# One more Strassen pair a round, a deeper ring of split weights, held pieces, and moved copies and loads in a float32 encoder layer

## The chip, the cores and the metric

The kernel runs on one core of one Trainium2 chip. The metric is the time of one execution on the device in microseconds; the median of 3 runs of the kernel before is 2016.77 us (2015.5 to 2017.98).

## The reference

One encoder layer on 256 tokens of width 2048 in float32: a feed-forward half-step, a mixer (attention and a Fourier branch), and a second feed-forward half-step. The change touches the two feed-forward blocks, and one place behind the first of them.

```python
def _swiglu(x, w_gate, w_up, w_down):
    return (jax.nn.silu(x @ w_gate) * (x @ w_up)) @ w_down

def _macaron_ffn(x, pre_g, w_gate, w_up, w_down, post_g):
    return x + MACARON_WEIGHT * _rms_norm(_swiglu(_rms_norm(x, pre_g), w_gate, w_up, w_down), post_g)
...
    h = _macaron_ffn(h, ffn1_pre_g[l], ffn1_w_gate[l], ffn1_w_up[l], ffn1_w_down[l], ffn1_post_g[l])
    h = _gated_mixers(h, ...)
    h = _macaron_ffn(h, ffn2_pre_g[l], ffn2_w_gate[l], ffn2_w_up[l], ffn2_w_down[l], ffn2_post_g[l])
```

D_MODEL is 2048 and D_FF is 5632, so each of `w_gate`, `w_up`, `w_down` holds 46 MB.

## The kernel before

**A product in three matmuls.** A float32 operand is split into a high and a low part: ScalarE (ACT) writes `whi`, the rounded value, and VectorE (DVE) writes `wlo`, the rest (`split`, L102 and L103). `mm3` (L108 to L110) then runs hi×hi, lo×hi and hi×lo on TensorE (PE). A weight piece is 128 partitions × 2 × 512 columns (`WP`, `NB`), 512 KB, loaded by SyncE's queue (SP) into one of 5 `raw` buffers. Its split goes into a ring of 6 places (`wring`, tiles `whi` and `wlo`).

**A round.** The hidden width is done in 11 blocks of 512 columns; the first two (`PLAIN`) by ordinary loops, the other nine in rounds (`ffn`, the loop over `f`). A round has two stages. In the row stage, 8 pieces r1 to r8 of `w_down` are multiplied with the block before (`Rows`; 12 matmuls a piece), added to the output `y` in this way: a copy of `y` is first written to a PSUM bank (`seed`, L637), the matmuls add onto it, and `out` copies it back (L655). In the product stage, gate and up of one block are computed (`swiglu`). The 2048 rows of the weights are 16 groups of 128, in 8 pairs. A pair that is done plainly takes 2 pieces and 8 products (24 matmuls). A pair in `BY_SEVEN` is done by Strassen's method with 7 products (21 matmuls): DVE forms three differences `t` and one in place of `raw` (`minus`, L557), and 4 pieces are split (three of 1024 elements a partition and one of 512). The names in the code for them are `first`, `second`, then `ra` and the half of `t`. Pairs 0, 1, 2, 4 and 6 are done so; 3, 5 and 7 plainly. Pair 5's two plain pieces stand between and behind the pieces of pair 4.

**The order** on DVE, ACT and PE inside the rounds is that of the code (`manual_schedule`). `Line` is a queue of steps: `feed` first runs as many of the oldest steps as needed to keep fewer than `RING` in the queue, then issues the split of the new piece. So piece n+6 is split behind the matmuls of piece n and behind whatever work hangs on step n (`then`). SP's order is set by a scheduler.

**A block's end.** When the sevens are done, their sums are read out of PSUM by adds on DVE (`add`, L562), then SiLU on ACT, `times` on DVE (L574), and the copies `seed(0)` and `seed(1)` of `y` for the next row stage, which need a PSUM bank each. There are 8 banks: 5 in the pool `pmm`, 3 in `ptr`. In the next row stage, the block is transposed (`turn_h`, PE tile `pt`), once a round.

**Memory.** Pool `b8` has 12 tiles of 8 KB a partition: in the rounds 2 for `y`, 6 for the split input (`Forms`, tiles `fh` and `fl`), and 4 that, in the kernel before, take from round f = 4 on the residual and the gains for the end of the block (`tail`: tiles `h`, `gpost`, `gpre`).

**Behind the first feed-forward.** `last_rows` ends the block: it normalises (`norm.scale`, tile `c`), adds the residual (`h`, L403), multiplies (`y`, L417), transposes and begins the next projection (`col`, PE tile `pc`). The mixer's constants are loaded at the same time: `tables` (L785, L788: tiles `gcq`, `gsq`, from `rc` and `rsn`) and the DFT matrices (`dps`, `dcs`, from `draw`).

Of the kernel before, what the change touches and what calls it, by code (L numbers as in the profile page):

```python
# [18 lines left out]
P = 128  # L19
# [24 lines left out]
RING = 6  # L44
SPARE = (None, None, "chunk", "u")
# [3 lines left out]
BY_SEVEN = (0, 1, 2, 4, 6)  # L49
# [7 lines left out]
def encoder_layer(  # L57
# [384 lines left out]
    class Forms:  # L442
# [3 lines left out]
        def __init__(self, u, rs):  # L446
            self.u, self.rs, self.seven, self.plain = u, rs, {}, {}
            self.rooms, self.used = [], KD

        def put(self, src):  # L450

            out, n = [], src.shape[1]
            while len(out) < n:
                if self.used == KD:
                    self.rooms, self.used = [big("f" + c, F32R, [P, KD, P]) for c in "hl"], 0
                a = len(out)
                m = min(n - a, KD - self.used)
# [40 lines left out]

    def ring(src):
# [11 lines left out]
    class Line:  # L511


        def __init__(self):
            self.queue = []
# [17 lines left out]
    def swiglu(line, forms, w, hs, seed):  # L533
# [13 lines left out]
        def plain(pair, i, *then):  # L547
# [6 lines left out]
            line.feed(lambda: ring(raw(pair, i)[:]), use, *then)  # L554
# [22 lines left out]
        def seven(pair, between=None, *then):  # L577
# [27 lines left out]
            if between:  # L605
                between()
            line.feed(lambda: ring(h["ra"][:]), two("p1", a11, "p6", s2, end), *then[0:2])
            line.feed(lambda: ring(h["t"][:, 0:1, :]), lambda ws: mul("g1", na22, ws[0]), *then[2:])

        sums = [copy, lambda: add("x2", "p6", "x1"), lambda: add("x3", "p7", "x2"), lambda: add("x2", "p5", "x2"),  # L610
                lambda: add("x5", "p5", "x3"), lambda: seed(0)]
        gates = [lambda: add("x1", "g0", "x1"), lambda: seed(1), lambda: add("x3", "g1", "x3"),
                 lambda: silu(0), lambda: silu(1)]
        ups = [lambda: add("x2", "u0", "x2"), lambda: times(0), lambda: add("x5", "u1", "x5"), lambda: times(1)]
        for kg in range(KD // CK):
            a, b = 2 * kg, 2 * kg + 1
            if kg == KD // CK - 1:
                seven(a, None, *sums)
                plain(b, 0, *gates)
# [8 lines left out]
    class Rows:  # L628
# [5 lines left out]
        def seed(self, cb, t):  # L634
            self.ps[cb, t] = pmm.tile([P, NB], F32, tag="mm", name="pr")
# [26 lines left out]
    def ffn(u, rs, wg, wu, wgu, wd, yname, tail, gate0, w_next=None, early=()):  # L662
# [668 lines left out]
```

## Time and profile before

| what | value |
|---|---|
| median of 3 runs | 2016.77 us |
| the profiled execution, whole | 2019.0 us |
| its span | 2017.2 us |
| granted TensorE clock, mean | 0.997 |
| PE busy (matmuls) | 1997.5 us |
| DVE busy | 1707.8 us |
| ACT busy | 1323.2 us |
| the 18 rounds, from transposition to transposition | 1132.95 us |

The profiled execution is 1.8 us longer than its span, and 2.2 us above the median. In the rows of a timeline the first column is the start, the second the duration (of all instructions of the row where it ends in xN), and the bracket names the idle time of that engine before the row and what ended it. A matmul's end is modelled; the distance from start to start is what PE really takes.

### The profile page before, as it was taken

To read this page: it belongs to the slowest core of one execution; us is meant where nothing else is said; L and a number is where in the kernel's file an instruction comes from. 1 tells how busy PE (TensorE), PEld (TensorE's weight loads), DVE (VectorE), ACT (ScalarE), POOL (GpSimd) and SP (SyncE) were. 2 spreads that over 40 slices of the span, in tenths; PEclk is the share of its full clock that TensorE was granted. 3 is DMA by queue.
4 is the path that set the end of the run, shared out by engine and by line. 5 is a ranking of instruction groups with operands and counts; after the bars stand their busy time and mean duration, and the time that the engine had idled before them with its cause. 6 is when DMAs were issued, how large, how long until landed. Compare 5 with 4: busy or idle time off the path is not lost.

```text
span 2017.2 us, 25972 instructions
## 1 busy us (share of the span) xinstructions
PE 1997.5 (99%) x9200; PEld 1654.6 (82%) x9200; DVE 1707.8 (85%) x2298; ACT 1323.2 (66%) x1898; POOL 28.6 (1%) x30
## 2 busy tenths in 40 slices
PE   9999999999999999999999999999999999999998
PEld 7888888888888878888888888878888888888886
DVE  6898899988999778886877885878998898988985
ACT  7567676676766856556676564656676776676766
POOL 0000000000000010100000000000000000000002
PEclk9999999999999999999999999999999999999999
DMA  8675665556655696954555557566755666556663
GB/s 316 216 255 187 206 221 199 192 187 203 221 201 192 228 292 193 266 189 137 189 193 186 193 166 276 197 210 199 249 180 195 195 225 208 182 194 197 223 206 115
DMA packets 118738, 417.44 MB, mean 207 GB/s; under 512 B 12968, under 2 KB 19120, under 8 KB 116432
## 3 DMA queue, kind: packets, MB, share of 16 engines
q1 hardware_dynamic: 114256, 411.66, 61.1%
q0 software_dynamic: 4352, 4.13, 1.4%
q8 instruction: 72, 1.18, 0.2%
q14 instruction: 58, 0.48, 0.1%
HBM read 409.44 MB, written 6.29 MB: 206 GB/s over the span
## 4 chain that ended last, share of the span: by engine, by line
PE 89%; DVE 7%; DMA 2%; ACT 1%; issue 1%; SPq 0%; DVEq 0%; ACTq 0%
PE pc L109 17%; PE pc L108 17%; PE pc L110 17%; PE pr L108 11%; PE pr L110 11%; PE pr L109 11%; DVE wlo L103 4%; PE pt L178 2%; DMA raw<-in_f_down 1%; DVE t L557 1%; ACT whi L102 1%; DMA raw<-in_w_fo 1%; DMA rc<-in_rope_cos 0%; PE pe L108 0%; PE pe L109 0%
## 5 line engine op out<-in xcount | busy, mean ns | idle before, releaser
L103 DVE TENSOR_TENSOR wlo<-raw,whi 128x1024 fp32r<-128x1024 f32 (+1 forms) x711 | 858.2, 1219 | 163.5 <-ACT whi L102 157.0
L102 ACT ACTIVATE whi<-raw 128x1024 fp32r<-128x1024 f32 (+1 forms) x711 | 742.1, 1055 | 330.7 <-PE pc L110 120.9
L108 PE MATMUL pc<-whi,fh 128*128 128x512 f32 x1062 | 413.1, 389 | 0.0
L109 PE MATMUL pc<-wlo,fh 128*128 128x512 f32 x1062 | 413.1, 389 | 0.0
L110 PE MATMUL pc<-whi,fl 128*128 128x512 f32 x1062 | 413.1, 389 | 0.0
L109 PE MATMUL pc<-wlo,uh 128*128 128x512 f32 x688 | 270.2, 393 | 3.9 <-DVE wlo L103 3.9
L108 PE MATMUL pc<-whi,uh 128*128 128x512 f32 x688 | 272.6, 396 | 0.9 <-ACT uh L739 0.9
L108 PE MATMUL pr<-whi,hTh 128*128 128x512 f32 x688 | 270.6, 393 | 0.5 <-ACT pr L637 0.4
L110 PE MATMUL pc<-whi,ul 128*128 128x512 f32 x688 | 270.0, 393 | 0.0
L110 PE MATMUL pr<-whi,hTl 128*128 128x512 f32 x688 | 268.0, 390 | 0.0
L109 PE MATMUL pr<-wlo,hTh 128*128 128x512 f32 x688 | 267.9, 389 | 0.0
L110 PEld LDWEIGHTS pc<-whi,fl 128*128 128x128 f32 x1062 | 199.3, 188 | 41.5
L108 PEld LDWEIGHTS pc<-whi,fh 128*128 128x128 f32 x1062 | 199.4, 188 | 41.4
L109 PEld LDWEIGHTS pc<-wlo,fh 128*128 128x128 f32 x1062 | 199.3, 188 | 41.3
L102 ACT ACTIVATE whi<-t 128x1024 fp32r<-128x1024 f32 (+1 forms) x180 | 152.2, 845 | 92.0 <-DVE t L557 91.6
L103 DVE TENSOR_TENSOR wlo<-t,whi 128x1024 fp32r<-128x1024 f32 (+1 forms) x180 | 171.5, 953 | 46.0 <-ACT whi L102 46.0
L557 DVE TENSOR_TENSOR t<-raw 128x512 f32<-128x512 f32 x270 | 178.1, 687 | 3.1
L109 PEld LDWEIGHTS pc<-wlo,uh 128*128 128x128 f32 x688 | 130.0, 189 | 30.3 <-DVE wlo L103 5.2
L108 PEld LDWEIGHTS pr<-whi,hTh 128*128 128x128 f32 x688 | 129.2, 188 | 30.0 <-ACT pr L637 3.8
L108 PEld LDWEIGHTS pc<-whi,uh 128*128 128x128 f32 x688 | 130.2, 189 | 28.0 <-ACT uh L739 2.3
L110 PEld LDWEIGHTS pc<-whi,ul 128*128 128x128 f32 x688 | 130.0, 189 | 27.0
L110 PEld LDWEIGHTS pr<-whi,hTl 128*128 128x128 f32 x688 | 129.1, 188 | 27.2
(331 smaller groups left out, 2180.1 us busy)
## 6 DMA issues: line engine op xcount, KB each, us to landing
raw<-in_f_gu SPq DMA_DIRECT2D x288, 512.0 KB, 4.1
raw<-in_f_down SPq DMA_DIRECT2D x176, 512.0 KB, 5.3
raw<-in_w_in SPq DMA_DIRECT2D x112, 512.0 KB, 4.6
raw<-in_f_up SPq DMA_DIRECT2D x32, 512.0 KB, 4.6
raw<-in_w_ao SPq DMA_DIRECT2D x32, 512.0 KB, 4.0
raw<-in_w_out SPq DMA_DIRECT2D x32, 512.0 KB, 4.2
raw<-in_f_gate SPq DMA_DIRECT2D x31, 512.0 KB, 5.8
fraw<-in_w_f SPq DMA_DIRECT2D x16, 512.0 KB, 6.4
```

The lines of the kernel that those rows point to most:

```text
L102: a = A.activation(hi, src, AF.Copy)
L103: v = V.tensor_tensor(out=lo, in0=src, in1=hi.bitcast(F32), op=ALU.subtract)
L108: T.matmul(ps, lh, rh, start=first, stop=False, skip_group_check=onto)
L109: T.matmul(ps, lh, rl, start=False, stop=False, skip_group_check=onto)
L110: return T.matmul(ps, ll, rh, start=False, stop=last, skip_group_check=onto)
L178: T.transpose(pt[:, j, :], src[:, j * P:(j + 1) * P], ident[:])
L557: V.tensor_tensor(out=out, in0=a, in1=b, op=ALU.subtract)
```

## The change

- **Pair 5 joins `BY_SEVEN`**: 6 of 8 pairs by seven products. The two left over products of the split input go to a tile `frest` of another pool.
- **Ring**: while `turn["more"]` is true (rounds f = 2 to 9 from their product stage on, and the row stage of f = 10), the queue holds 10 steps, and 4 of every 10 pieces go to a `b8` tile `w2` that holds both parts. The product stage of f = 10 and all behind it has 6 places again.
- **Tail loads**: since those four tiles are in use, `tail` is called at the last round's end instead of at f = 4.
- **Hold**: `feed` keeps steps unprepared while the step executed last was marked `hold`; marked are the last two steps of the last seven pair and the first plain step of pair 7. So no new piece is split between these steps' `then` work.
- **Copies**: `seed(0)` takes a bank of `ptr` (the one that `p1` leaves) right behind the copy of `p1`, and `seed(1)` stands right behind the first add. Four items of `sums` now hang on the last seven's third piece instead of two.
- **Tables**: the 12 small DVE instructions of `tables` are placed behind the split that was issued last.

```diff
+RING_B8 = 4
-BY_SEVEN = (0, 1, 2, 4, 6)
+BY_SEVEN = (0, 1, 2, 4, 5, 6)
...
+                    if self.full <= 3:
+                        self.rooms, self.used, self.size = [big("f" + c, F32R, [P, KD, P]) for c in "hl"], 0, KD
+                    else:
+                        rest = xpool.tile([P, 4, P], F32R, tag="xt", name="frest")
...
     def ring(src):
-        hi = wring.tile([P, WP, NB], F32R, tag="hi", name="whi")
-        lo = wring.tile([P, WP, NB], F32R, tag="lo", name="wlo")
+
         n = src.shape[1]
+        i = turn["n"] = (turn["n"] + 1) % (RING + RING_B8)
+        if turn["more"] and i % 5 in (1, 3):
+            both = big("w2", F32R, [P, 2, WP, NB])
+            hi, lo = both[:, 0], both[:, 1]
+        else:
+            hi = wring.tile([P, WP, NB], F32R, tag="hi", name="whi")
+            lo = wring.tile([P, WP, NB], F32R, tag="lo", name="wlo")
         split(hi[:, 0:n, :], lo[:, 0:n, :], src)
...
-        def feed(self, ready, use, *then):
-
-            while len(self.queue) >= RING:
+        def feed(self, ready, use, *then, hold=False):
+
+
+            while len(self.queue) >= RING + RING_B8 * turn["more"]:
                 self.next()
-            self.queue.append((ready(), use, then))
+            self.queue.append([ready, use, then, hold])
+            if not self.held:
+                self.prepare()
+
+        def prepare(self):
+            for step in self.queue:
+                if step[0]:
+                    weights, step[0] = step[0](), None
+                    step[1] = lambda use=step[1], weights=weights: use(weights)
 
         def next(self):
-            b, use, then = self.queue.pop(0)
-            use(b)
+            if self.queue[0][0]:
+                self.prepare()
+            _, use, then, self.held = self.queue.pop(0)
+            use()
...
-            line.feed(lambda: ring(h["ra"][:]), two("p1", a11, "p6", s2, end), *then[0:2])
-            line.feed(lambda: ring(h["t"][:, 0:1, :]), lambda ws: mul("g1", na22, ws[0]), *then[2:])
-
-        sums = [copy, lambda: add("x2", "p6", "x1"), lambda: add("x3", "p7", "x2"), lambda: add("x2", "p5", "x2"),
-                lambda: add("x5", "p5", "x3"), lambda: seed(0)]
-        gates = [lambda: add("x1", "g0", "x1"), lambda: seed(1), lambda: add("x3", "g1", "x3"),
-                 lambda: silu(0), lambda: silu(1)]
+            line.feed(lambda: ring(h["ra"][:]), two("p1", a11, "p6", s2, end), *then[0:4], hold=end)
+            line.feed(lambda: ring(h["t"][:, 0:1, :]), lambda ws: mul("g1", na22, ws[0]), *then[4:], hold=end)
+
+        sums = [copy, lambda: seed(0, ptr, "tr"), lambda: add("x2", "p6", "x1"), lambda: seed(1),
+                lambda: add("x3", "p7", "x2"), lambda: add("x2", "p5", "x2"), lambda: add("x5", "p5", "x3")]
+        gates = [lambda: add("x1", "g0", "x1"), lambda: add("x3", "g1", "x3"), lambda: silu(0), lambda: silu(1)]
...
-                plain(b, 0, *gates)
+                plain(b, 0, *gates, hold=True)
...
-                if f == 4:
+                if f == nblk:
                     norm, nxt = tail(y)
...
+                    turn["more"] = f < nblk - 1
...
-                V.tensor_tensor(out=gc[:, t, :], in0=rc[:, t, :], in1=g[:], op=ALU.mult)
+                with tc.issue_after(latest["V"]):
+                    V.tensor_tensor(out=gc[:, t, :], in0=rc[:, t, :], in1=g[:], op=ALU.mult)
```

Three places show how instructions move. The first is DVE at a block's end in the first feed-forward, before the change; `x` are the sums, `raw` the next pieces, `t` a difference of the next block.

```order
L562 TENSOR_TENSOR x_3111<-pc,x_3109 128x512
L103 TENSOR_TENSOR wlo<-raw,whi 128x1024
L562 TENSOR_TENSOR x_3122<-pc,x_3111 128x512
L562 TENSOR_TENSOR x_3111<-pc,x_3111 128x512
L562 TENSOR_TENSOR x_3125<-pc,x_3122 128x512
L103 TENSOR_TENSOR wlo<-raw,whi 128x1024
L562 TENSOR_TENSOR x_3109<-pc,x_3109 128x512
L562 TENSOR_TENSOR x_3122<-pc,x_3122 128x512
L103 TENSOR_TENSOR wlo<-raw,whi 128x1024
L562 TENSOR_TENSOR x_3111<-pc,x_3111 128x512
```

The same engine and place with the change:

```order
L587 TENSOR_TENSOR x_3121<-pc,x_3117 128x512
L587 TENSOR_TENSOR x_3128<-pc,x_3121 128x512
L587 TENSOR_TENSOR x_3121<-pc,x_3121 128x512
L587 TENSOR_TENSOR x_3131<-pc,x_3128 128x512
L587 TENSOR_TENSOR x_3117<-pc,x_3117 128x512
L587 TENSOR_TENSOR x_3128<-pc,x_3128 128x512
L587 TENSOR_TENSOR x_3121<-pc,x_3121 128x512
L599 TENSOR_TENSOR x_3121<-x_3121,x_3117 128x512
L587 TENSOR_TENSOR x_3131<-pc,x_3131 128x512
L599 TENSOR_TENSOR x_3131<-x_3131,x_3128 128x512
L104 TENSOR_TENSOR w_3167<-raw,w_3167 128x1024
L104 TENSOR_TENSOR wlo<-raw,whi 128x1024
```

The splits of new pieces between the sums have moved behind the last of them. The second place is SP's queue in the first feed-forward before the change, from the load of the first round's `w_down` on:

```order
L83 DMA raw<-in_f_down 128x1024 x8
L83 DMA raw<-in_f_gu 128x1024 x3
L83 DMA h_1975<-in_x 128x2048
L83 DMA raw<-in_f_gu 128x1024 x2
L83 DMA h_1977<-in_x 128x2048
L83 DMA raw<-in_f_gu 128x1024 x2
L83 DMA gpost_1979<-in_f_post 128x2048
L83 DMA gpre_1981<-in_mix_pre 128x2048
L83 DMA raw<-in_f_gu 128x1024 x9
```

SP's queue with the change, from the `w_down` load of round f = 10 on:

```order
L84 DMA raw<-in_f_down 128x1024 x8
L84 DMA raw<-in_f_gu 128x1024 x3
L84 DMA h_5790<-in_x 128x2048
L84 DMA h_5792<-in_x 128x2048
L84 DMA gpost_5794<-in_f_post 128x2048
L84 DMA raw<-in_f_gu 128x1024 x2
L84 DMA gpre_5796<-in_mix_pre 128x2048
L84 DMA raw<-in_f_gu 128x1024 x11
L84 DMA raw<-in_f_down 128x1024 x16
```

The four tail loads have moved from the weights of the first round to those of the last one; each waits there for a `w2` tile that PE still reads. The third place is DVE behind the first feed-forward, before the change, from the last steps of the norm's root (`cu`, `cv`, `cr`) on:

```order
L165 TENSOR_TENSOR cu<-cz 128x1
L785 TENSOR_TENSOR gcq<-rc,gq 128x128
L166 SCALAR_TENSOR_TENSOR cv<-cu,ca 128x1
L785 TENSOR_TENSOR gcq<-rc,gq 128x128
L168 SCALAR_TENSOR_TENSOR cr<-cv,cz 128x1
L103 TENSOR_TENSOR wlo<-raw,whi 128x1024
L403 SCALAR_TENSOR_TENSOR h_1977<-y_935,cr,h_1977 128x512
L103 TENSOR_TENSOR dps<-draw,dps 128x258
L417 TENSOR_TENSOR y_935<-h_1977,gpre_1981 128x512
```

The same with the change:

```order
L166 TENSOR_TENSOR cu<-cz 128x1
L167 SCALAR_TENSOR_TENSOR cv<-cu,ca 128x1
L169 SCALAR_TENSOR_TENSOR cr<-cv,cz 128x1
L104 TENSOR_TENSOR wlo<-raw,whi 128x1024
L404 SCALAR_TENSOR_TENSOR h_5792<-y_942,cr,h_5792 128x512
L104 TENSOR_TENSOR dps<-draw,dps 128x258
L418 TENSOR_TENSOR y_942<-h_5792,gpre_5796 128x512
```

The `gcq` products have left this stretch (they stand some 40 instructions later, behind the roots `r0r` and `r1r`); the split of `dps` still stands ahead of `y`.

More of the change, by code (lines that the diff above doesn't have):

```diff
@@ L545, in raw, with plain @@
             return raw_piece(w[pair // 2], pair % 2 * 2 + i)
-        def plain(pair, i, *then):
+        def plain(pair, i, *then, hold=False):
             def use(b):
@@ L552, in use @@
                         mul("gu"[i] + str(t), forms.plain[k][t], b[j], k == KD - 1)
-            line.feed(lambda: ring(raw(pair, i)[:]), use, *then)
+            line.feed(lambda: ring(raw(pair, i)[:]), use, *then, hold=hold)
         def minus(out, a, b):
```

23 lines of the change are left out of this document (13 added, 10 removed).

## The prediction

> **What bounds the kernel now.** I read the page's head first, then the busy times by round, then the starts of single instructions inside a round, and last the waits.
>
> ```profile
> span 2017.2 us, 25972 instructions
> PE 1997.5 (99%) x9200; PEld 1654.6 (82%) x9200; DVE 1707.8 (85%) x2298; ACT 1323.2 (66%) x1898; POOL 28.6 (1%) x30
> ...
> PEclk9999999999999999999999999999999999999999
> ```
>
> PE is covered for 99% of the span, DVE for 85%, and the granted clock is full nearly everywhere. A covered PE is not yet a bound PE, since ends of matmuls are modelled, so the starts decide.
>
> ```profile
> 450.63 0.39 PE L110 MATMUL pc<-whi,fl 128*128 128x512 f32 x1
> ...
> 454.94 0.39 PE L108 MATMUL pc<-whi,fh 128*128 128x512 f32 x1
> ```
>
> These are the first and last of 20 matmuls in the product stage of a round: 4.31 us over 19 steps, so one matmul costs 0.2268 us of PE and not the 0.39 us of its row. Next the rounds, cut at their transpositions.
>
> ```profile
> core 0: us, PE busy (x) PEld busy (x) DVE busy (x) ACT busy (x) POOL busy (x), PEclk, DMA share, GB/s
> 112.08:174.88 62.80, 62.80 (x284) 52.06 (x282) 57.80 (x68) 43.54 (x55) 0.00 (x0) 1.00 0.71 244
> ...
> 300.75:363.54 62.79, 62.79 (x284) 52.07 (x282) 56.61 (x66) 43.43 (x55) 0.00 (x0) 1.00 0.59 201
> ...
> 615.46:678.48 63.02, 63.02 (x284) 52.00 (x282) 54.47 (x62) 44.35 (x57) 0.00 (x0) 1.00 0.61 209
> ...
> 1915.98:1979.26 63.28, 63.07 (x284) 52.01 (x282) 54.47 (x62) 44.24 (x57) 0.00 (x0) 1.00 0.63 204
> sum 1132.95, PE 1132.48 PEld 936.59 DVE 1017.85 ACT 784.07 POOL 0.00; mean PE 62.92 PEld 52.03 DVE 56.55 ACT 43.56 POOL 0.00
> ```
>
> A round has 32 + 35 + 24 products of three matmuls, 273 in all: 61.9 us at 0.2268, and 0.9 us is left for its 8 transpositions. So 62.79 us is PE's own time, and the 18 rounds together lie only 1132.95 − 18 × 62.79 = 2.73 us above it. The rounds are PE-bound. DVE has 56.6 us of work in 62.8.
>
> The Trainium skill ("Perfetto Trace Analysis", Identifying the Most-Contended Engine) says that matmul busy time does not tell the headroom of TensorE, and that weight-load busy time and the other engines' occupancy do; by that rule the round's 52.0 us of weight loads stand behind DVE's 56.6, DVE is the most contended engine, and a change that takes from PE and gives to DVE loses. The 0.2268 us from start to start speak against it here; it returns as the second rival.
>
> **Removed: 54 matmuls.** Pair 5 needs 21 matmuls instead of 24 in each of 18 rounds: 54 × 0.2268 = 12.2 us off PE, which is on the path. A round's PE time becomes 62.79 − 0.68 = 62.11 us.
>
> **Added: work on DVE and ACT.** The stretch of pair 4 (by seven) and pair 5 (plain) on DVE in one round:
>
> ```profile
> 446.75 1.29 DVE L557 TENSOR_TENSOR t<-raw 128x512 f32<-128x512 f32 x2
> 447.96 1.22 DVE L103 TENSOR_TENSOR wlo<-raw,whi 128x1024 fp32r<-128x1024 f32 x1
> 449.10 0.68 DVE L557 TENSOR_TENSOR raw<-raw,t 128x512 f32<-128x512 f32 x1
> 449.70 1.22 DVE L103 TENSOR_TENSOR wlo<-t,whi 128x1024 fp32r<-128x1024 f32 x1
> 450.95 0.69 DVE L557 TENSOR_TENSOR t<-raw 128x512 f32<-128x512 f32 x1
> 451.56 2.35 DVE L103 TENSOR_TENSOR wlo<-raw,whi 128x1024 fp32r<-128x1024 f32 x2
> 453.83 0.68 DVE L103 TENSOR_TENSOR wlo<-t,whi 128x512 fp32r<-128x512 f32 x1
> 454.43 1.22 DVE L103 TENSOR_TENSOR wlo<-raw,whi 128x1024 fp32r<-128x1024 f32 x1
> 455.57 1.29 DVE L557 TENSOR_TENSOR t<-raw 128x512 f32<-128x512 f32 x2
> ```
>
> From 446.75 to 455.57 are 8.82 us for one seven and two plain splits. A plain split takes (453.83 − 451.56)/2 = 1.135 us, so a seven takes 6.55, and pair 5 by seven adds 6.55 − 2.27 = 4.28 us to DVE: 60.9 us in a round of 62.1. ACT has 62.8 − 43.4 = 19 us idle in each round, and its one and a half more splits hide there. DVE's room shrinks from 6.2 to 1.2 us; whether that suffices depends on when it may work ahead, which is the ring's business.
>
> **Ring of 10, middle rounds.** PE consumes a seven in 21 × 0.2268 = 4.8 us and DVE makes one in 6.55, so in the product stage DVE falls behind and lives on what is ready at its start. Where PE and DVE stood late in the stage before the change:
>
> ```profile
> 434.33 1.23 DVE L103 TENSOR_TENSOR wlo<-t,whi 128x1024 fp32r<-128x1024 f32 x1 [1.44 <-ACT whi L102]
> ...
> 456.77 1.22 DVE L103 TENSOR_TENSOR wlo<-raw,whi 128x1024 fp32r<-128x1024 f32 x1
> ...
> 460.37 1.22 DVE L103 TENSOR_TENSOR wlo<-raw,whi 128x1024 fp32r<-128x1024 f32 x1
> ```
>
> ```profile
> 432.50 0.39 PE L108 MATMUL pc<-whi,fh 128*128 128x512 f32 x1
> ...
> 462.42 0.39 PE L108 MATMUL pc<-whi,fh 128*128 128x512 f32 x1
> ```
>
> The stage starts at 432.50. The split that ends at 435.56 is piece 6, the first one held up by the copies at the end of the row stage. The last seven is needed at 462.42 and its first piece is ready at 457.99: 4.4 us of slack; its third piece, ready at 461.59 and needed 12 matmuls later, at 465.14, has 3.55. With 10 places the piece so held up is the tenth. Counted from the stage's start: tenth piece 3.06; the rest of pairs 2 and 3, 0.61 + 3 × 1.135 + 0.60 = 4.6; two sevens 13.1; the last seven's first piece 2.43. That is ready at 23.2, and PE, after 129 matmuls, wants it at 29.3. The slack is 6 us in place of 4.4, although there is one seven more. So I charge nothing for the middle rounds.
>
> **Ring of 6, last rounds.** In the product stage of f = 10 of each feed-forward there are 6 places again but six sevens. Slack 3.55 − 4.28 − 0.68 = −1.4 us: PE waits 1.4 us there, in two rounds. Bounds: 0, if DVE enters that stage earlier, to 4, if its pieces start late.
>
> **Hold, copies.** Behind a hold nothing is split until the last plain piece is multiplied: the pieces queued behind it on DVE and ACT are r7, r8 and the next block's first two with 10 places, and r3 to r6 with 6. With 10, r1 to r6 (6 × 12 × 0.2268 = 16 us of PE) cover that. With 6, r1 and r2 cover 5.4 us, and the sums left (4 × 0.6 us) and r3's split (1.2 us) need 3.6. So hold costs nothing, and the adds and the copies come earlier. What that is worth:
>
> ```profile
> PEld pr L108 <- ACT pr L637: 3.8, 9, 0.6
> ```
>
> In 9 of 18 rounds the row stage's weight load waited for a copy of `y`, which waited for the adds. These waits make the 2.73 us. In the 16 rounds other than the last ones I take 2.73 − (0.23 + 0.49) = 2.0 us as gone. In the last two the 0.72 goes too, under the 1.4 us each: +2.1.
>
> **Tail loads.** 4 MB in the first feed-forward (3 in the second) move from the first round to the last.
>
> ```profile
> raw<-in_f_gu SPq DMA_DIRECT2D x288, 512.0 KB, 4.1
> ...
> h<-in_x SPq DMA_DIRECT2D x2, 1024.0 KB, 8.6
> ...
> gpre<-in_mix_pre SPq DMA_DIRECT2D x1, 1024.0 KB, 10.0
> ```
>
> SP now waits for PE: `gpost` for a `w2` tile that r3 frees and `gpre` for one that r5 frees, with the product stage's weights queued behind them on SP. r5 ends some 9 us before that stage (3 × 2.72 and the transpositions), and the raw pieces behind `gpre` serve the third pair, whose multiplication starts 42 × 0.2268 = 9.5 us into it; landing takes 10.0 + 4.1 and splitting 2.4, 16.5 of 18.5 us. So it fits, with 2 us to spare. Before, the same bytes in the first round (244 GB/s there against 201) cost PE nothing. I charge 0; bounds 0 and 4 us for each feed-forward.
>
> **Tables.** The one long wait of PE near the change lies behind the first feed-forward:
>
> ```profile
> 718.28 0.29 DVE L785 TENSOR_TENSOR gcq<-rc,gq 128x128 f32<-128x128 f32 x1 [3.01 <-DMA rc<-in_rope_cos]
> ...
> 720.87 0.43 DVE L103 TENSOR_TENSOR dps<-draw,dps 128x258 fp32r<-128x258 f32 x1 [0.16 <-ACT dps L102]
> 721.22 0.69 DVE L417 TENSOR_TENSOR y<-h,gpre 128x512 f32<-128x512 f32 x1
> ```
>
> ```profile
> 720.42 0.42 ACT L102 ACTIVATE dps<-draw 128x258 fp32r<-128x258 f32 x1 [8.66 <-DMA draw<-in_dft_pos]
> ```
>
> ```profile
> 720.10 0.79 PE L109 MATMUL pc<-wlo,uh 128*128 128x512 f32 x1 [3.26 <-DVE wlo L103]
> ...
> 722.83 0.83 PE L178 MATMUL pt<-ident,y 128*128 128x128 f32 x4
> ```
>
> ```profile
> 720.10:722.83 2.73, 2.73 (x7) 2.04 (x8) 2.57 (x4) 1.85 (x6) 0.00 (x0) 0.50 0.77 161
> ```
>
> DVE waits 3.01 us for `rc`, and the split behind it keeps PE waiting 3.26 us. The change takes `gcq` away, but not its neighbour: `dps` waits for its own load until 720.42 on ACT, its DVE half still stands ahead of `y`, so `y` ends at 721.9 as before. PE gets its wlo early, does six matmuls (1.4 us), and waits at the transposition of `y` until 721.9 instead of 722.83: 0.9 us gained at best. After the old wait the granted clock was 0.50 for 2.7 us, six matmuls at twice their price. The new wait is some 3.9 us long, so that slow stretch comes behind it and takes the 0.9 back. I charge 0, with bounds −0.9 and +0.9.
>
> The Trainium skill ("TensorE: Matmul & The Clock Gate", What's actually happening) puts the halved clock down to an idle window of about 3.4 us; the trace agrees (0.50 behind 3.3 us), and by that rule only a wait made clearly shorter, not one moved, would give the 1.4 us of slow matmuls back, for a sum 1.4 us lower.
>
> The split input's three more products for pair 5, once for each feed-forward, fall into the second plain block:
>
> ```profile
> 37.00:112.00 75.00, 75.00 (x338) 62.04 (x337) 62.16 (x95) 46.58 (x62) 0.00 (x0) 1.00 0.68 228
> ```
>
> PE is covered there without a gap and DVE has 13 of 75 us idle: 0, and 2 us if that cover fails.
>
> **Sum.** −12.2 − 2.0 + 2.1 + 0 = −12.1 us. The profiled execution, 2019.0 us with a span of 2017.2, would become 2006.9; from the median of the runs, 2016.77, it is 2004.6.
>
> **Rivals.** 0.2% (4 us) is about what a measurement of this kernel can tell from no change.
>
> 1. *All waits of PE in the rounds go*, because DVE enters the last rounds 1.4 us earlier: 12.2 + 2.73 + 0.9 gives 2000.9. For it: the ring is still full when f = 10 begins. Against: its product stage starts behind the same copies as before. Chance 0.13.
> 2. *DVE becomes the bound in every round.* If the 6.2 us that DVE now idles in a round come from its back-and-forth with ACT and remain, a round takes 60.9 + 6.2 = 67.1 us, 4.3 more in each of 18: 2094. The point from which it is slower than before: more than 62.8 − 60.9 = 1.9 us of DVE idle a round. For it: the rows show waits for ACT (1.44 above). Against: from 446.75 to 455.57 DVE ran without a gap, so the idle time lies where the ring was full. Chance 0.08, slower.
> 3. *The last rounds starve*, because SP stands behind PE with the tail loads: 4 us more in each feed-forward, 2012.6. For it: only 2 us to spare. Against: the first round bore the same loads. Chance 0.11, about half of it within 0.2%.
> 4. *The change doesn't do what it says*: the saved matmuls turn up as waits at each block's end, and a round stays near 62.8: 2015. Against: six microseconds of slack. Chance 0.05, within 0.2%.
>
> **Chances and range.** My forecast has 0.63. Faster: 0.63 + 0.13 + 0.06 = 0.82; within 0.2%: 0.05 + 0.05 = 0.10; slower 0.08. The forecast's own range is 2001.5 to 2009 (last rounds 0 to 4 us, tables ±0.9). The range given reaches to the first rival and to the third, 2000 to 2012.5.
>
> **What would show it.** Middle rounds of 62.1 us, with DVE near 61 and the waits of weight loads for L637's copies gone: right. Last rounds near 63.5: the −1.4 is right; 66 or more with SP behind `h` or `gpre`: the third rival. A wait for `y` of 3 to 4 us near 718 instead of one for wlo: the tables' step is right. Rounds of 64 us and more with waits for wlo all over: the second rival, and the forecast is wrong.

## Result: 6.3% slower

The changed kernel takes 2142.69 us (median of 4 runs, 2140.42 to 2148.34), the kernel before 2017.09 in the runs beside it: a ratio of 1.0628, 95% interval 1.0606 to 1.065. The prediction, 2004.6 us (2000.0 to 2012.5), was wrong in sign and in size.

The page of the changed kernel, its head and first part:

```profile
span 2146.6 us, 26154 instructions
...
PE 2032.8 (95%) x9146; PEld 1669.9 (78%) x9146; DVE 1790.8 (83%) x2416; ACT 1360.3 (63%) x1940; POOL 28.6 (1%) x30
```

PE runs 54 matmuls fewer (9146 for 9200), as planned, and yet its busy time rose from 1997.5 to 2032.8 us, while its share of the span fell from 99% to 95%. So there are waits, and matmuls that take longer. Rounds cut at their transpositions (columns: stretch and length, busy time and count of each engine, granted clock, DMA share, GB/s), and in the second row the 8 us behind one of the waits:

```profile
core 0: us, PE busy (x) PEld busy (x) DVE busy (x) ACT busy (x) POOL busy (x), PEclk, DMA share, GB/s
400.41:471.96 71.55, 65.31 (x279) 53.19 (x278) 61.21 (x72) 45.59 (x57) 0.00 (x0) 0.95 0.53 177
456.00:464.00 8.00, 5.64 (x13) 4.44 (x14) 7.18 (x10) 5.66 (x10) 0.00 (x0) 0.57 0.63 214
615.03:677.19 62.16, 62.16 (x280) 51.49 (x278) 54.13 (x64) 41.95 (x53) 0.00 (x0) 1.00 0.70 240
677.19:741.95 64.76, 63.29 (x279) 51.20 (x278) 57.92 (x69) 45.03 (x58) 0.00 (x0) 1.00 0.62 210
```

The third of these rows has no wait, and it shows PE's own time of a round: 62.16 us, the 62.11 of the prediction. It is the round in which the ring goes back from 10 places to 6 and DVE prepares little. The first row is an ordinary round: 62.16 + 3.15 of slow matmuls (65.31 − 62.16) + 6.24 without PE = 71.55. The first round of each feed-forward, in which the ring grows from 6 to 10 places, has two such waits and takes 76.3 us. The nine rounds of the first feed-forward:

```profile
112.22:741.95 629.73, 582.81 (x2503) 475.59 (x2502) 548.17 (x646) 410.64 (x517) 0.00 (x0) 0.95 0.55 188
```

629.73 us against 566.40 before (112.08 to 678.48). The second feed-forward's nine take 630.85 (1477.56 to 2108.41) against 566.55. Together that is 127.6 of the 129.4 us by which the span grew. What PE waits for there (in total, times, longest):

```profile
PE pr L109 <- ACT pr L661: 91.9, 19, 6.1
PE pt L179 <- DVE y L418: 4.1, 1, 4.1
PE pc L110 <- DVE wlo L104: 1.8, 7, 0.4
```

Not for split weights (`wlo`: 1.8 us in all) but for the copies of `y` into PSUM banks, once in most rounds. Here is one of these waits, in the rows of PE, ACT and DVE (start, duration, in brackets the idle time before and what ended it). L591 copies P1, the product that the block's sums begin with; L595 are the two silus; L661 the copies of `y`:

```profile
440.06 0.39 PE L109 MATMUL pc<-w,fh 128*128 128x512 f32 x1
...
451.86 0.39 PE L111 MATMUL pr<-whi,hTl 128*128 128x512 f32 x1
458.36 0.79 PE L109 MATMUL pr<-w,hTh 128*128 128x512 f32 x1 [6.11 <-ACT pr L661]
```

```profile
442.95 1.06 ACT L103 ACTIVATE whi<-raw 128x1024 fp32r<-128x1024 f32 x1 [2.04 <-DMA raw<-in_f_down]
...
445.21 0.58 ACT L591 ACTIVATE x<-pc 128x512 f32<-128x512 f32 x1
...
449.84 1.23 ACT L595 ACTIVATE x<-x 128x512 f32<-128x512 f32 x2 [2.04 <-DVE x L587]
...
456.76 1.06 ACT L103 ACTIVATE whi<-t 128x1024 fp32r<-128x1024 f32 x1 [2.85 <-DVE t L582]
457.72 1.10 ACT L661 ACTIVATE pr<-y 128x512 f32<-128x512 f32 x2
```

```profile
433.47 0.68 DVE L104 TENSOR_TENSOR w<-t,w 128x512 fp32r<-128x512 f32 x1
...
445.33 1.23 DVE L104 TENSOR_TENSOR w<-raw,w 128x1024 fp32r<-128x1024 f32 x1
446.48 4.53 DVE L587 TENSOR_TENSOR x<-pc,x 128x512 f32<-128x512 f32 x7
```

P1's product is complete at the latest when the next piece's matmuls begin, at 440.06. From there PE has work until 452.25 (458.36 less the wait of 6.11; the rest of the block, r1 and r2): 12.2 us of cover. But ACT copies P1 only at 445.21, 5.15 us late, because the pieces up to r6 stand ahead of that copy in its queue (on DVE they end at 446.56). And from that copy to PE's restart it takes 13.15 us: sums, silus, then the burst behind the hold, whose fourth piece waits 2.85 us on ACT for DVE's difference `t`, and only behind it the copies for the second column block. 5.15 + 13.15 is 18.3 us, 6.1 more than the cover, so PE waits, and afterwards the clock is halved for a while (the granted 0.57 of the row from 456.00).

### The profile page after: what moved, and what is told of

Same layout as the page of the kernel before. It is cut to its first block, busy times and chain, and to the rows that moved or that the text cites. A ratio compares the mean times of both kernels' runs of the same rounds, so it can differ in the third digit from the quotient of the medians.

```text
span 2146.6 us, 26154 instructions
## 1 busy us (share of the span) xinstructions
PE 2032.8 (95%) x9146; PEld 1669.9 (78%) x9146; DVE 1790.8 (83%) x2416; ACT 1360.3 (63%) x1940; POOL 28.6 (1%) x30
## 4 chain that ended last, share of the span: by engine, by line
PE 62%; DVE 25%; DMA 5%; ACT 4%; issue 3%; SPq 0%; DVEq 0%; ACTq 0%
PE pc L110 11%; PE pc L111 11%; PE pc L109 11%; DVE wlo L104 10%; PE pr L109 8%; PE pr L110 8%; PE pr L111 8%; DVE t L582 4%; DVE w L104 4%; DVE x L587 3%; DMA raw<-in_f_down 3%; ACT whi L103 2%; DVE raw L582 1%; PE pt L179 1%; ACT x L595 1%
## 5 line engine op out<-in xcount | busy, mean ns | idle before, releaser
L104 DVE TENSOR_TENSOR wlo<-raw,whi 128x1024 fp32r<-128x1024 f32 (+1 forms) x560 | 677.1, 1219 | 152.9 <-ACT whi L103 150.3
L103 ACT ACTIVATE whi<-raw 128x1024 fp32r<-128x1024 f32 (+1 forms) x560 | 585.3, 1055 | 298.6 <-PE pc L111 126.8
L109 PE MATMUL pr<-whi,hTh 128*128 128x512 f32 x492 | 206.3, 419 | 63.7 <-ACT pr L661 63.5
L110 PE MATMUL pc<-wlo,fh 128*128 128x512 f32 x626 | 244.4, 390 | 1.2 <-DVE wlo L104 1.0
L109 PE MATMUL pc<-whi,fh 128*128 128x512 f32 x626 | 243.9, 390 | 0.7 <-DVE hTl L104 0.7
L111 PE MATMUL pc<-whi,fl 128*128 128x512 f32 x626 | 243.8, 389 | 0.0
L104 DVE TENSOR_TENSOR w<-raw,w 128x1024 fp32r<-128x1024 f32 x151 | 184.3, 1220 | 29.1 <-ACT w L103 28.5
L103 ACT ACTIVATE w<-raw 128x1024 fp32r<-128x1024 f32 x151 | 159.2, 1054 | 68.7 <-DMA raw<-in_f_down 21.9
L111 PE MATMUL pr<-whi,hTl 128*128 128x512 f32 x492 | 200.9, 408 | 0.0
L110 PEld LDWEIGHTS pc<-wlo,fh 128*128 128x128 f32 x626 | 117.5, 188 | 27.9 <-DVE wlo L104 3.7
L109 PEld LDWEIGHTS pc<-whi,fh 128*128 128x128 f32 x626 | 117.5, 188 | 26.0 <-issue 0.8
```

The source lines that it names most:

```text
L103: a = A.activation(hi, src, AF.Copy)
L104: v = V.tensor_tensor(out=lo, in0=src, in1=hi.bitcast(F32), op=ALU.subtract)
L109: T.matmul(ps, lh, rh, start=first, stop=False, skip_group_check=onto)
L110: T.matmul(ps, lh, rl, start=False, stop=False, skip_group_check=onto)
L111: return T.matmul(ps, ll, rh, start=False, stop=last, skip_group_check=onto)
```

## The experiments

**The theories.** From that trace came theory A: the burst behind the hold is the cause, since it stands ahead of the copies. It fell with the first four runs, and theory E took its place: ACT and DVE run their work in the order of the code, and with R places whatever they do for a step stands behind the preparation of the piece R steps further on; a deeper ring puts more preparation ahead of the sums and copies, and a sixth seven gives DVE more to do there. The rivals: B, DVE's amount of work is the bound; C, the banks; D, the burst on DVE; G, POOL and DVE block each other; L, the loads.

### No hold

```diff
         def feed(self, ready, use, *then, hold=False):
+            hold = False
```

> The changed kernel with hold never set; ring of 10, sixth seven, banks and tables stay. Theory A (the four held pieces are prepared in one burst on ACT ahead of the copies of y for the second column block, and PE waits about 6 us for these, after which its clock is low): the rounds fall from 70-72 to 62.2-62.6 us, the last ones stay near 64.8; time 2008 to 2016 us. Rival B (DVE, with six sevens, is the bound, hold or not): rounds stay above 66 us, time above 2090. Rival C (the copies in other banks cause the wait): rounds stay near 71, 2140.

Measured: 2142.34 us, ratio 1.0609 (1.0588 to 1.0631). Nothing is won, and theory A as it stood is refuted. The time is also the one that rival C gave for the changed banks; C falls with a later version that has the same banks, no wait for a copy, and 2010.6 us. ACT's rows in a round of this kernel, and PE's wait:

```profile
367.89 0.58 ACT L592 ACTIVATE x<-pc 128x512 f32<-128x512 f32 x1
...
376.41 1.23 ACT L596 ACTIVATE x<-x 128x512 f32<-128x512 f32 x2 [4.00 <-DVE x L588]
...
379.43 1.10 ACT L662 ACTIVATE pr<-y 128x512 f32<-128x512 f32 x2
```

```profile
380.06 0.79 PE L109 MATMUL pr<-whi,hTh 128*128 128x512 f32 x1 [5.16 <-ACT pr L662]
```

The same splits now stand one by one between the sums (the silus wait 4.00 us for DVE's sums in place of 2.04), not in a burst behind them. P1's copy is as late as before, and 12.2 us follow it in place of 13.15.

### Copies of the second column block ahead of the burst

```diff
-        gates = [lambda: add("x1", "g0", "x1"), lambda: add("x3", "g1", "x3"), lambda: silu(0), lambda: silu(1)]
+        gates = [lambda: add("x1", "g0", "x1"), lambda: add("x3", "g1", "x3"), lambda: silu(0), lambda: silu(1),
+                 lambda: seed(0, cb=1), lambda: seed(1, cb=1)]
...
-                        self.seed(cb + 1, t)
+                        if (cb + 1, t) not in self.ps:
+                            self.seed(cb + 1, t)
```

> The changed kernel, hold kept; the copies of y for the second column block are issued on ACT right behind the two silus, ahead of the burst, instead of by r1's step. Theory A: the order of ACT is all, so the wait of 6 us goes though hold stays: rounds 62.2 to 63, time 2008 to 2018. Rival B: no change, above 2090. A rival D to A (DVE's burst of splits behind the release is the brake, not the copies): PE then waits for wlo of r7/r8 or for the next copies instead, rounds 66 or more, above 2080.

Measured: 2103.22 us, 1.0419 (1.0403 to 1.0435); rounds of 67.7 to 68.7 us, but for the first of each feed-forward (72.2) and the last two. A (2008 to 2018) is out, and so is B's "no change", since 39 us are won by moving two copies a round alone. D's forecast came true: PE waits for the next copies instead, in rounds above 66. The wait moved by one column block.

```profile
375.43 1.06 ACT L103 ACTIVATE whi<-t 128x1024 fp32r<-128x1024 f32 x1 [1.80 <-DVE t L582]
...
379.59 1.12 ACT L662 ACTIVATE pr<-y 128x512 f32<-128x512 f32 x2
```

```profile
380.24 0.50 PE L109 MATMUL pr<-whi,hTh 128*128 128x512 f32 x1 [3.67 <-ACT pr L662]
```

The copies for the second block are now in time. Those for the third, at 379.59, stand behind the next pieces that need `t`, and PE waits 3.67 us for them. So D's burst on DVE and the order on ACT are one cause here: theory E takes in both.

### Five sevens in the changed kernel

```diff
-BY_SEVEN = (0, 1, 2, 4, 5, 6)
+BY_SEVEN = (0, 1, 2, 4, 6)
```

> The changed kernel with pair 5 plain again: 273 matmuls a round, DVE 4.3 us less work; hold, ring of 10, banks, tables stay. Theory A: the burst is the same four pieces, so the wait stays and the round is 62.8 + 8 to 9 us: time 2140 to 2160, no faster than the changed kernel. Rival B: DVE has its room back, rounds near 62.8 and time near 2017.

Measured: 2054.5 us, 1.0183 (1.0166 to 1.02). Between both: faster by 88 us than the changed kernel, slower by 36 than the kernel before although it does the same products. A round:

```profile
374.64:439.04 64.40, 63.11 (x283) 51.99 (x282) 57.16 (x66) 43.69 (x55) 0.00 (x0) 1.00 0.59 197
```

```profile
414.82 0.58 ACT L591 ACTIVATE x<-pc 128x512 f32<-128x512 f32 x1
...
426.38 1.06 ACT L103 ACTIVATE whi<-t 128x1024 fp32r<-128x1024 f32 x1 [2.85 <-DVE t L582]
427.34 1.10 ACT L661 ACTIVATE pr<-y 128x512 f32<-128x512 f32 x2
```

```profile
427.98 0.50 PE L109 MATMUL pr<-w,hTh 128*128 128x512 f32 x1 [1.29 <-ACT pr L661]
```

The burst and its 13.16 us are the same (414.82 to 427.98), but P1 is now copied in time, and the wait shrinks to 1.29 us. So the two parts add: the burst behind the ring of 10 costs what its 13.2 us are above the cover (11.7 us here, from 414.96, where the next piece's matmuls begin, to 1.29 us before 427.98), and the sixth seven adds the delay of P1's copy. Of the 36 us, some 15 lie in the first rounds of the two feed-forwards, which take 69.5 and 71.2 us.

### A ring of 6 in all rounds

```diff
-RING_B8 = 4
+RING_B8 = 0
...
-        if turn["more"] and i % 5 in (1, 3):
+        if False:
```

> The changed kernel with a ring of 6 in all rounds, hold kept. The burst is then r3 to r6, which hold no piece that DVE must first make (no t). Theory A: the copies come behind four splits on ACT, PE waits about 1 us as in the last rounds, which had 6 places; with the 1.7 us for DVE there, rounds of 64 to 66 us: time 2030 to 2075. If hold cost the wait whatever stands in the burst: rounds of 70 and more, above 2130.

Measured: 2050.23 us, 1.016 (1.0145 to 1.0175); rounds of 64.8 us, as expected.

```profile
349.43 0.58 ACT L591 ACTIVATE x<-pc 128x512 f32<-128x512 f32 x1
...
355.48 3.88 ACT L103 ACTIVATE whi<-raw 128x1024 fp32r<-128x1024 f32 x4
359.27 1.10 ACT L661 ACTIVATE pr<-y 128x512 f32<-128x512 f32 x2
```

```profile
359.90 0.50 PE L109 MATMUL pr<-whi,hTh 128*128 128x512 f32 x1 [1.00 <-ACT pr L661]
```

The burst is four plain splits without a wait, 10.5 us from P1's copy to PE's restart. That is less than the cover, and PE waits 1.00 us only because P1's copy is late here too (the next piece's matmuls begin at 347.15, 2.3 us before it). The four places, meant to help, cost 92 us (2142.7 to 2050.2). A round is still 2.6 us above 62.16. The copies make 1.0 of that, and the rest comes with DVE: the weight loads' waits show 35.1 us for `wlo` in 59 places.

```profile
PEld pc L110 <- DVE wlo L104: 35.1, 59, 1.4
```

### Without the copies of y

```diff
-            self.w, self.rb, self.y, self.first, self.ps = w, rb, y, first, {}
+            self.w, self.rb, self.y, self.first, self.ps = w, rb, y, True, {}
+            self.write = first
...
-                for t in range(NT):
+                for t in range(NT if self.write else 0):
                     A.activation(cbs(self.y[t], cb), self.ps[cb, t][:], AF.Copy)
```

> The changed kernel (hold, ring of 10, six sevens) without the copies of y from and to the banks in all rounds but the first of each feed-forward: the row products start afresh, and their sums are lost. Theory E (the in-order queue: with 10 places, whatever ACT and DVE do for a step stands behind the preparation of a piece ten steps ahead; at a block's end DVE has that preparation still before it, and so the copies come late and PE waits for them): without the copies the waits of 5 to 6 us go, the clock stays at 1.00, rounds of 62.2 to 64 us, time 2010 to 2045. Rival B (DVE's amount of work is the bound): PE waits for wlo instead, rounds above 66, time above 2085.

Measured: 2035.23 us, 1.0089 (1.0075 to 1.0104), inside theory E's range. With all of DVE's work, the ring of 10 and the hold, 107 of the 126 us go with the copies. Their own work goes with them (ACT's busy time in a round falls from 45.6 to 36.9 us), but ACT had some 26 us of idle time in a round before. Fourteen of the 18 rounds take 62.1 to 63.7 us; the other four, 64.7 to 67.3, are longer than expected. A round, and the wait that is left, for P1's own copy:

```profile
433.25:496.83 63.58, 62.40 (x279) 51.37 (x278) 60.64 (x73) 36.89 (x41) 0.00 (x0) 1.00 0.58 200
```

```profile
PE pr L109 <- ACT x L591: 16.5, 12, 2.2
```

### The longer ring alone, on the kernel before

`ring`, the length of the queue and the tail's place as in the change:

```diff
+RING_B8 = 4
...
-            while len(self.queue) >= RING:
+            while len(self.queue) >= RING + RING_B8 * turn["more"]:
...
-                if f == 4:
+                if f == nblk:
```

> The kernel before (five sevens, no hold, its banks and tables) with a ring of 10 and the tail's loads in the last round, nothing else. Theory E: the longer ring alone makes it slower, since the sums and copies come behind pieces four steps further on: rounds of 63.5 to 65, time 2030 to 2060. If the loss with five sevens (2054.5) came from hold or from the banks: 2017, within 0.3%.

Measured: 2034.18 us, 1.0091 (1.0072 to 1.011): inside theory E's range, but not in the way it gave. Sixteen rounds take 62.8 to 63.8 us, most of them below the 63.5 to 65 expected, and 11 of the 16 us that the rounds lose lie in the first round of each feed-forward (68.1 and 68.5 us), where the ring grows. So the sign and the kind of wait are shown, and that the time fits is partly luck. In its rounds the weight loads' waits for copies have grown from 3.8 us in 9 cases to

```profile
PEld pr L109 <- ACT pr L646: 19.1, 26, 3.8
```

### The sixth seven alone, on the kernel before

```diff
-BY_SEVEN = (0, 1, 2, 4, 6)
+BY_SEVEN = (0, 1, 2, 4, 5, 6)
```

`Forms` takes `frest` as in the change.

> The kernel before (ring of 6, no hold) with the sixth pair by seven products, nothing else. If DVE's 4.3 us a round fit into its idle time, rounds of 62.1 to 62.5 and 2004 to 2011. Theory E with DVE as the bound at 6 places: rounds of 64 to 66 us as in ring_of_six, with waits for wlo; time 2035 to 2070, slower than before by more than the saved 12 us are worth.

Measured: 2118.78 us, 1.0504 (1.049 to 1.0518). Slower than theory E gave by 49 us at least. A ring of 6 without hold has splits between the sums, as in the kernel before; with DVE later, the copy that r1 needs comes late, and a halved clock, which the expectation had not counted, comes behind the wait:

```profile
434.97 0.50 PE L108 MATMUL pr<-whi,hTh 128*128 128x512 f32 x1 [2.33 <-ACT pr L642]
...
435.65 0.63 PE L110 MATMUL pr<-whi,hTl 128*128 128x512 f32 x1
436.08 0.63 PE L108 MATMUL pr<-whi,hTh 128*128 128x512 f32 x1
```

From 435.65 the matmuls start 0.43 us apart. Against this, the ring of six with hold takes 2050.2 us, 69 less; its banks, the order of its copies and its tables differ too, so the 69 us are not hold's alone.

### Hold alone, on the kernel before

`Line` as in the change, and at the three last steps but one of a block:

```diff
-            line.feed(lambda: ring(h["ra"][:]), two("p1", a11, "p6", s2, end), *then[0:2])
-            line.feed(lambda: ring(h["t"][:, 0:1, :]), lambda ws: mul("g1", na22, ws[0]), *then[2:])
+            line.feed(lambda: ring(h["ra"][:]), two("p1", a11, "p6", s2, end), *then[0:2], hold=end)
+            line.feed(lambda: ring(h["t"][:, 0:1, :]), lambda ws: mul("g1", na22, ws[0]), *then[2:], hold=end)
...
-                plain(b, 0, *gates)
+                plain(b, 0, *gates, hold=True)
```

> The kernel before (ring of 6, five sevens) with hold, nothing else. Theory E: the burst behind the hold is r3 to r6, four splits on ACT (3.9 us) ahead of the copies for the second column block; PE waits 0.1 to 1.0 us a round for these, in place of the 0.15 before: rounds of 62.8 to 63.8, time 2015 to 2036. My prediction's view (hold is free and ends the waits for copies): 2014 to 2016.

Measured: 2015.35 us, 0.999 (0.9981 to 0.9999). By the time alone this also lies at the lower edge of theory E's range, but E's 0.1 to 1.0 us of waits a round do not come, and the prediction's view holds here. A round is PE's own time, with no wait for copies left:

```profile
363.14:425.91 62.77, 62.77 (x282) 52.11 (x281) 57.06 (x67) 43.07 (x55) 0.00 (x0) 1.00 0.59 202
```

That fits the rows of the ring of six: 10.5 us from P1's copy on, when that copy is not late, lie under 11.7 us of cover.

### Two subtractions of each seven on POOL

`minus` gets the engine as an argument (VectorE unless said otherwise); the first of the two kernels has `RING_B8 = 0` too.

```diff
-minus(t[:, 1, :], rb[:, 0, :], ra[:, 1, :])
+minus(t[:, 1, :], rb[:, 0, :], ra[:, 1, :], nc.gpsimd)
...
-minus(h["t"][:, 0, :], h["ra"][:, 1, :], h["rb"][:, 1, :])
+minus(h["t"][:, 0, :], h["ra"][:, 1, :], h["rb"][:, 1, :], nc.gpsimd)
```

> The ring of 6 with hold and six sevens, and two of the subtractions of each seven (0.6 us each on DVE) on POOL, where a product of two 128x512 tensors took 1.31 us. DVE's work falls from 61.2 to some 54 us a round. Theory E, with DVE as the bound at 6 places (rounds of 64.8): rounds of 62.2 to 63, time 2006 to 2022. Rival G (POOL and DVE keep each other waiting when both read two tensors; the Trainium skill, SBUF - State Buffer, SBUF: two separate sides, states such a lock): the 12 subtractions of 1.31 us stop DVE, rounds of 66 or more, time above 2075.

> The changed kernel (ring of 10, hold) with the same two subtractions of each seven on POOL. Theory E: DVE's lag at the end of a block shrinks by more than five sevens did (rounds of 64.4 with 56.6 us of DVE), but the copies still stand behind pieces that need t: rounds of 63 to 65, time 2020 to 2055, slower than six_pool. Rival B: DVE was all, so it equals six_pool. Rival G: above 2142.

Measured: 2181.93 us, 1.0817 (1.0802 to 1.0831) with 6 places, and 2244.15, 1.1124 (1.1108 to 1.114) with 10, as rival G gave. The groups of instructions of the former, then the second group as it is in the ring of six without POOL:

```profile
L582 POOL TENSOR_TENSOR t<-raw 128x512 f32<-128x512 f32 x216 | 388.0, 1804 | 1519.1 <-DMA raw<-in_f_gu 1172.8 <-DVE wlo L104 315.2 <-PE pc L111 24.4
```

```profile
L104 DVE TENSOR_TENSOR wlo<-raw,whi 128x1024 fp32r<-128x1024 f32 x709 | 925.3, 1325 | 183.6 <-ACT whi L103 175.4 <-ACT yA L224 0.3
```

```profile
L104 DVE TENSOR_TENSOR wlo<-raw,whi 128x1024 fp32r<-128x1024 f32 x709 | 849.8, 1219 | 113.9 <-ACT whi L103 109.7 <-PE pr L111 2.0
```

A subtraction on POOL takes 1804 ns, not 1313, and DVE's splits grow from 1219 to 1325 ns on average; the longest takes 2327 ns, against 1228 without POOL. On DVE the round below is busy for 60.92 us, about as in two rounds of the ring of six without POOL (61.1 on average), although it runs 12 instructions fewer.

```profile
398.00:469.75 71.75, 65.87 (x280) 50.65 (x278) 60.92 (x61) 45.26 (x59) 21.52 (x12) 1.00 0.50 176
```

So these subtractions, moved to POOL, did not relieve DVE. How much of the loss is the mutual blocking and how much POOL's own slowness is not separated: a subtraction of 1.8 us in place of 0.6 stands in the chain of a piece too, and ACT waits 227 us in total for POOL's `t` in the kernel with 6 places.

### Half the loads

```diff
+    def half_piece(src, i):
+        raw = wraw.tile([P, WP, NB], F32, tag="raw", name="raw")
+        load(raw[:, 0:1, :], src.rearrange("p (i k c) -> p i k c", k=WP, c=NB)[:, i, 0:1, :])
+        return raw[:, 0:1, :].to_broadcast([P, WP, NB])
...
-                    line.feed(lambda i=i, cb=cb: ring(raw_piece(self.w[self.rb, cb], i)[:]),
+                    line.feed(lambda i=i, cb=cb: ring(half_piece(self.w[self.rb, cb], i)),
```

> The changed kernel with half the bytes of each piece of in_f_down loaded in the rounds (256 KB in place of 512; the other half repeats the first, so the products are of other weights), splits and matmuls as they were. In the changed kernel the copy of x1 starts 5.0 us after its product, and 4.0 us of ACT's time ahead of it are waits for loads of in_f_down. If the loads are the cause of that delay (rival L): it falls to some 2 us, PE's wait from 6.1 to 3 or less, the clock stays high, rounds of 62.5 to 66 us, time 2015 to 2075. If DVE's work is (theory E in its strict form): delay and wait stay, time 2110 to 2145.

Measured: 2092.54 us, 1.0375 (1.036 to 1.039): between both ranges, so neither rival is the whole.

```profile
427.08 0.57 ACT L596 ACTIVATE x<-pc 128x512 f32<-128x512 f32 x1
```

```profile
425.49 0.39 PE L109 MATMUL pc<-w,fh 128*128 128x512 f32 x1
...
440.56 0.50 PE L109 MATMUL pr<-w,hTh 128*128 128x512 f32 x1 [3.35 <-ACT pr L666]
```

From 427.08 to 440.56 are 13.5 us, nearly as before; P1's product was complete at 425.49, where the next piece's matmuls begin, so its copy is 1.6 us late in place of 5.15. So the loads make some 3.5 us of that delay in this round (the rows of the changed kernel show 2.04 us of it a little ahead of P1's copy), as rival L gave. But the wait is 3.35 us and not 3 or less, and the clock still falls behind most such waits: the rest is the order behind P1's copy.

### Versions with early copies, a ring of 6, and the tables put behind

The place behind the first feed-forward by itself, on the kernel before: the tables and the splits of `dps` and `dcs` are issued behind the transpositions of `y`, on ACT too.

```diff
+    with tc.issue_after(latest["A"]):
         dps = const.tile([P, 2, WE + WO], F32R, name="dps")
         split(dps[:, 0, :], dps[:, 1, :], constant(dft_pos, WE + WO)[:])
...
```

The lines up to `mid` (with `dcs`, `odd`, `first` and `alt`) stand in the same block, and the products of `tables` are placed as in the change.

> The kernel before with the tables gcq, gsq, gck, gsk and the splits of dps and dcs behind the transpositions of y, on DVE and on ACT; the rounds are untouched. PE's wait of 3.3 us behind the first feed-forward and the slow 2.7 us after it (1.4 us of loss) go: 2011 to 2014. If only the wait moves again (to h, y or uh): 2015 to 2018.

Measured: 2013.52 us, 0.9984 (0.9975 to 0.9993). No wait of PE there is longer than 0.41 us.

> Five sevens, ring of 6, hold, the changed kernel's banks, the copies of the second column block ahead of the burst, and the tables and dps behind the transpositions. Theory E: without the longer ring and the sixth seven nothing that DVE must first make stands ahead of the copies; rounds of 62.8, no waits for copies: 2008 to 2013, faster than both kernels. If hold still costs its 1.0 us a round (as in ring_of_six): 2026 to 2032.

> Like five_early_six, with six sevens: ring of 6, hold, copies of the second column block ahead of the burst, tables and dps behind the transpositions. Theory E: the 1.0 us of waits for copies a round in ring_of_six goes, and 4 us behind the first feed-forward; the waits for wlo, which DVE's amount of work sets, stay: rounds of 63.5 to 64, time 2022 to 2036, slower than five_early_six by 0.6 to 1.3%. If the sixth seven were free once the copies come early: 62.2 a round, 1998 to 2004.

Measured: with five sevens **2010.61 us, 0.9969 (0.9958 to 0.998)**, faster than both kernels; with six 2036.4, 1.0098 (1.0081 to 1.0115), 0.4 us above what was expected. The tables behind the transpositions, alone, had given 3.6 of the 6.5 us that the former gains on the kernel before, and hold alone 1.8. A round of the former and one of the latter:

```profile
363.05:425.82 62.77, 62.77 (x283) 52.09 (x281) 57.07 (x67) 43.34 (x55) 0.00 (x0) 1.00 0.59 202
```

```profile
303.41:367.29 63.88, 63.10 (x280) 51.18 (x278) 60.61 (x73) 44.15 (x58) 0.00 (x0) 1.00 0.58 196
```

Where hardly a copy is late, the sixth seven still costs (2036.4 − 2010.6)/18 = 1.4 us a round: PE saves its 0.68, and some 2.1 us come in its place, with DVE busy for 61 us in 64. The longest sum of weight loads' waits is for `wlo` (37.0 us); 6.6 us are still for the copies. This price stayed with the best order of the copies that was tried.

## Why the prediction was wrong

The eight kernels with and without each part, in us (the four with a star have the change's banks and tables too):

| | 5 sevens | 6 sevens |
|---|---|---|
| 6 places, no hold | 2017.1 (before) | 2118.8 |
| 6 places, hold | 2015.4 | 2050.2* |
| 10 places, no hold | 2034.2 | 2142.3* |
| 10 places, hold | 2054.5* | 2142.7* (the change) |

- *Removed: 54 matmuls.* Right: the round without waits takes 62.16 us.
- *Added: work on DVE.* The amount was right (busy 61.2 us against the 60.9 forecast), but not that 1.2 us of room would do with a ring that lets it work ahead. No kernel with six sevens came below 2035, and with 6 places and no hold the sixth seven alone cost 102 us. The rule of the Trainium skill ("Perfetto Trace Analysis", Identifying the Most-Contended Engine), by which the prediction found DVE the engine to spare, gave the right sign here. It is no test of the rule, which names the share of peak FLOPs (MFU) beside weight-load time for TensorE, and the prediction left that out.
- *Ring of 10, middle rounds, charged 0.* **This is the step that failed.** Its 6 us of slack are in the trace: the last seven's first piece is ready at 429.95 and wanted at 435.98, its last at 434.15 (433.47 + 0.68) and 440.06. But they are the slack of the pieces, and DVE isn't free in them. It goes on with pair 7's pieces and r1 to r6 (and waits 0.88 and 1.87 us for ACT in between, which waits for loads), and the sums, which with 10 places stand behind r6, start at 446.48. The prediction followed the split weights through the ring and did not ask where in the same queues the sums and copies stand. What the step put at nothing is the larger part of the loss: with hold and six sevens the four places cost 92 us.
- *Hold, copies.* Right with 6 places and five sevens (no wait for a copy is left). Wrong with 10: it set 16 us of cover (r1 to r6) against the held pieces, but the copies for the second column block are queued behind them on ACT and wanted after r2.
- *Ring of 6, last rounds*: 64.76 and 65.01 us against 63.5. The step's direction was right, the size short by 1.3 us; 1.01 us of it is a wait for a copy (at 730.93), which hold was to end.
- *Tail loads*: 0 was right as far as seen. The last round behind them (64.76) is as long as the rounds with 6 places and no such loads (64.8 in the ring of six).
- *Tables*: right. The wait of PE moved to the transposition of `y`, which waits for `dps`, which waits on ACT; the forecast was 3 to 4 us, and some 3.9 in its working:

```profile
786.40 1.08 PE L179 MATMUL pt<-ident,y 128*128 128x128 f32 x4 [4.06 <-DVE y L418]
```

```profile
785.23 0.43 DVE L104 TENSOR_TENSOR dps<-draw,dps 128x258 fp32r<-128x258 f32 x1 [3.94 <-ACT dps L103]
```

- *Rival 2* (DVE bound, 67.1 us a round, 2094) had the right sign, with a chance of 0.08. Its mark, waits for `wlo` all over, did not show in the changed kernel (1.8 us; 6.5 us of weight loads' waits, where the ring of six has 35.1). DVE's lateness reached PE by way of ACT's copies instead, and the slow clock after each wait, 3.15 us a round, was in no rival.
- *The range.* The forecast's own 2001.5 to 2009 does not follow from the bounds named with it: last rounds of 0 to 4 us and ±0.9 for the tables give 2000.9 to 2010.7. Nothing hangs on it.

What stays open: how the delay of P1's copy divides between DVE and the loads was tried at one size of load only, and more buffers for loads were not tried.

## What to carry to other kernels

In an engine that runs in order, a deeper prefetch is not only more buffers: it puts more work ahead of every short operation that someone waits for, so for each such copy or sum write down what stands in front of it and by when it is wanted. Slack of the prefetched data is not slack of the engine that makes it. An engine at 57 us of 63 with a chain of hand-overs behind it is already near its bound; put the short operations first, as the version of 2010.6 us does (3.6 of its 6.5 us come from the tables), before adding to it.

## Of the hardware, not expected

- A wait of PE of some 2 us could be enough to halve the clock, and one of 3.4 us could leave it full. In the kernel without the copies, matmuls came 0.43 us apart in place of 0.2268 behind a wait of 2.13 us (granted clock 0.50 from 161.50 to 164.50); with the longer ring alone they came 0.23 apart behind a wait of 3.40 us (granted clock 1.00 from 1473.88 on):

```profile
161.50 0.80 PE L109 MATMUL pr<-whi,hTh 128*128 128x512 f32 x1 [2.13 <-ACT x L591]
```

```profile
1473.88 0.50 PE L109 MATMUL pr<-whi,hTh 128*128 128x512 f32 x1 [3.40 <-ACT pr L646]
```

Behind the rounds' waits for copies of 1.00 and 1.29 us it stayed full, and behind those of more than 3.5 it always fell. Between 2.1 and 3.4 us the length of the wait does not decide, and what does is not shown. The prediction had cited the Trainium skill ("TensorE: Matmul & The Clock Gate", What's actually happening) for an idle window of about 3.4 us; by these rows a shorter wait could be enough.
- POOL and DVE slowed each other when both worked on two float32 tensors: 1804 ns for a subtraction on POOL, where a product of the same form took 1313 elsewhere, and 1325 for 1219 on DVE. The Trainium skill ("SBUF — State Buffer", SBUF: two separate sides) states a lock that the two hold for a whole instruction; the trace agrees that single instructions are held up (2327 ns for a split that takes 1228 at most without POOL), and shows no lock as such.
